# A gated trunk's start, its norm and its banded scores: loads in another order, sums on another engine, rows of 128

## The chip, the cores and the metric

The kernel runs on one core of a Trainium2 chip. The metric is the device time of one execution in microseconds. Engines are named as in the profile: PE is TensorE, DVE VectorE, ACT ScalarE, POOL GpSimd and SP the engine that issues nearly all DMAs. PEld is TensorE's loading of weights, which overlaps its products.

## The reference

Two layers over 512 positions of 1024 features. Each normalises x, modulates it, projects it, runs three causal token mixers side by side, gates and merges them:

```
mod = silu(c) @ w_ada + b_ada;  shift, scale, gate = split(mod, 3)
u = rms_norm(x, norm_g) * (1 + scale) + shift
z = u @ w_in                                 # all mixers' q, k, v and gates
ya = top-k sparse attention (8 heads, rotary, indexer of 4 heads, top 128)
yb = sliding window of 128, 8 q heads on 2 kv heads, sinks in the softmax, rotary
yc = stick-breaking attention (8 heads)
merged = sum_b sigmoid(m_b) * ((y_b * silu(gate_b)) @ w_br_b)
x = x + gate * (merged @ w_out)
```

and a last rms_norm follows. In the banded mixer (b) a block of 128 queries sees its own and the previous block of keys.

## The kernel before

**Tiling.** Features lie on the 128 partitions, positions along the row, so x is eight chunks of 128 x 512 in two tiles, `vc` (chunks 0 to 3) and `va` (4 to 7). Each product of full precision is three of fp32r: a value is split in a high and a low part (u into `uh` and `ul`, weights into `whi` and `wlo`), and hi·hi, hi·lo and lo·hi are summed in PSUM. The first block of a layer (`first_phase`) takes the eight chunks one after another and fills seven banks: 7 x 3 products a chunk. In layer 0, chunks 0 and 1 are worked in halves of 256 positions, 7 x 3 x 2 x 2 = 84 short products, and chunks 2 to 7 whole, 126 products of 512 columns.

**The start** (`start`, with `norm`, `ada_load`, `ada_first`). Before that block, x must be loaded, squared, summed over features (`nones` is a matrix of -1 that sums over partitions), and turned into 1/rms by Ln and Exp on ScalarE; silu(c) is spread into `csr`; and for each chunk j two dot products of 1024 elements (shift and scale: `Y` tiles of w_ada against `csr`, on VectorE) give `mods` and `amul`. `times_rstd` scales x in place and `make_u` makes uh, a copy e and ul. `norm` is called for positions 0 to 255 and again for 256 to 511. Loads go through four `wstage` tiles for weights and five `Y` tiles.

**Who orders the work.** Instructions are recorded by `Recorder.add`, which finds dependencies from the bytes that a view spans (`View.region`: from the lowest to the highest byte), and placed by `Recorder.forward`, a list scheduler: it walks forward in time with a price for each operation, picks an engine where several are allowed (`rec.add` with a dict), and takes the instruction with the earliest start, then the earliest due time of the round before. The best of five rounds is emitted. So every engine's order, SP's queue of loads too, follows from recorded dependencies and prices. All instructions are recorded on one line (549; 547 for products on 64 rows).

**Banded scores** (`softmax_qk`, b = "b"). For a pair of heads the queries lie in `Q`, high part on 64 partitions and low part on the other 64; `kb` is a pair of KH tiles, high and low keys, each with the same 64 rows on both halves. Four blocks of queries by two heads give eight products on 128 rows (high keys against high and low queries) and then, in one run (`low_parts` with `LOW_BAND`), eight on 64 rows (low keys against high queries), two of them side by side on the array. There are four pairs in each of two layers: eight groups.

Of the kernel before, what the change touches and what calls it, by code (L numbers as in the profile page):

```python
# [25 lines left out]
F32 = mybir.dt.float32  # L26
F32R = mybir.dt.float32r
BF16 = mybir.dt.bfloat16
AF = mybir.ActivationFunctionType
OP = mybir.AluOpType  # L30

D = 1024
S = 512
P = 128
# [119 lines left out]
class View:  # L154
# [30 lines left out]
    def real(self):  # L185
# [2 lines left out]
            ap = ap.rearrange(arg, a=more[0]) if more else getattr(ap, name)(arg)  # L188
        return ap

    def region(self):

        whole = self.tile.at
        p0, f0 = divmod(self.at.__array_interface__["data"][0] - whole.__array_interface__["data"][0], whole.shape[1])
        free = list(zip(self.at.strides[1:], self.at.shape[1:]))
        lo = f0 + sum(min(0, s * (n - 1)) for s, n in free)
        hi = f0 + sum(max(0, s * (n - 1)) for s, n in free) + 1
        return p0, p0 + self.at.shape[0], lo, hi
# [45 lines left out]
class Recorder:  # L244
# [29 lines left out]
    def add(self, ways):  # L274
        x = Instr()
        x.i = len(self.list)
        op, args, kw = next(iter(ways.values()))
        if op == "pairs":
            named = [(("out", "in", "in")[n], v) for q in args for n, v in enumerate(q)]
        else:  # L280
            named = [("out" if "out" not in kw and n == 0 else n, v) for n, v in enumerate(args)] + list(kw.items())
        x.writes = [v for n, v in named if isinstance(v, View) and n in ("out", "accum_out")]
        x.reads = [v for n, v in named if isinstance(v, View) and n not in ("out", "accum_out")]
        x.preds, x.succs = {}, []
        for views, w in ((x.reads, False), (x.writes, True)):
            for v in views:
                t, r = v.tile, v.region()
                if op == "matmul" and w and kw["start"]:
                    r = (r[0], r[1], 0, S)
                keep = []  # L290
                for (j, r2, w2) in t.seen:
                    over = r[0] < r2[1] and r2[0] < r[1] and r[2] < r2[3] and r2[2] < r[3]
                    if over and j is not x and (w or w2):
                        x.preds[j.i] = j
                    if not (w and over and r[0] <= r2[0] and r2[1] <= r[1] and r[2] <= r2[2] and r2[3] <= r[3] and j is not x):
                        keep.append((j, r2, w2))
                t.seen = keep + [(x, r, w)]
        x.tiles = list({id(v.tile): v.tile for v in x.reads + x.writes if not v.tile.pool.fixed}.values())
        for j in x.preds.values():
            j.succs.append(x)  # L300
        x.alts = {}
        for e, (op, args, kw) in ways.items():
            x.alts[e] = self.price(x, e, op, args, kw)
        x.prio = x.i
        self.list.append(x)
# [266 lines left out]
def trunk(ctx, tc, xT, vecs, w_ss, w_gt, w_first, w_t, w_v, w_br, w_o, rope, consts, out):  # L572
# [24 lines left out]
    def mm(o, lhsT, rhs, start, stop=True):  # L597
        PE.matmul(o, lhsT, rhs, start=start, stop=stop, skip_group_check=True)
# [5 lines left out]
    f = lambda ap: ap.bitcast(F32)  # L604
# [14 lines left out]
    def both(out, a, b, op_):  # L619
        how = ("tensor_tensor", (), dict(out=out, in0=a, in1=b, op=op_))  # L620
        rec.add({"DVE": how} if in_psum(a, b) else {"POOL": how, "DVE": how})
# [12 lines left out]
    csb, o = small[:, 0:8], 8  # L634
    g_sb = [small[:, o + 8 * l:o + 8 * l + 8] for l in range(L)]
    fg_sb, o = small[:, o + 8 * L:o + 8 * L + 8], o + 8 * L + 8
    b_ada, o = [small[:, o + 24 * l:o + 24 * l + 24] for l in range(L)], o + 24 * L
    sink, o = small[:, o:o + 8 * L], o + 8 * L
    ident = small[:, o:o + P]
    nones = fixed("nones", [P, P], F32R)  # L640
# [56 lines left out]
    st = {}  # L697


    mods = [fixed(f"mods{l}", [P, 24], F32) for l in range(L)]  # L700
    amul = [fixed(f"amul{l}", [P, 8], F32) for l in range(L)]
# [21 lines left out]
    def ada_first(j):  # L723
        o = rec.tile("dot", [P, 4], F32)
        for i in range(2):
            w, m = st["wada", j][i], 8 * i + j
            DVE.scalar_tensor_tensor(w, w, 1.0, csr, op0=OP.mult, op1=OP.mult, accum_out=o[:, i:i + 1])
            DVE.tensor_tensor(out=mods[0][:, m:m + 1], in0=o[:, i:i + 1], in1=b_ada[0][:, m:m + 1], op=OP.add)
        DVE.scalar_tensor_tensor(amul[0][:, j:j + 1], mods[0][:, 8 + j:9 + j], 1.0, g_sb[0][:, j:j + 1], op0=OP.add, op1=OP.mult)

    def ada_g(l, j, q):
        def fn(w):
# [35 lines left out]
    def make_u(l, k, xk, cs_=FULL):  # L768
        t = t512("e", 2)[:, cs_]
        sc, sh = amul[l][:, k:k + 1], mods[l][:, k:k + 1]  # L770
        if cs_.start == 0:
            st["uh"][k] = t512(f"uh{k}", 1, F32R)
            st["ul"][k] = t512(f"ul{k}", 1, F32R)
        for o in (st["uh"][k][:, cs_], t):
            rec.add({"ACT": ("activation", (o, xk[:, cs_], AF.Identity), dict(scale=sc, bias=sh)),
                     "DVE": ("tensor_scalar", (o, xk[:, cs_], sc, sh), dict(op0=OP.mult, op1=OP.add))})
        both(st["ul"][k][:, cs_], t, f(st["uh"][k][:, cs_]), OP.subtract)
# [278 lines left out]
    def low_parts(q, kl, pos, banks, b, order):  # L1056

        quads = []
        for e, i in order:
            k0, W = keys(b, i)  # L1060
            bk, c0 = pos(e, i)
            hp = (H0, H1)[e]
            quads.append((banks[bk][:, c0:c0 + W], q[hp, e, 128 * i:128 * i + 128], kl[hp, k0:k0 + W]))
        pairs(quads)

    LOW_ALL = ((0, 3), (1, 3), (0, 2), (1, 2), (0, 1), (1, 0), (0, 0))
    LOW_BAND = ((0, 2), (1, 2), (0, 3), (1, 3), (0, 1), (1, 1), (0, 0), (1, 0))

    def c_qk(p):
        def fn():  # L1070
# [62 lines left out]
    def softmax_qk(b, p):  # L1133
        def fn():
            q = st[f"{b}q{p}"]
# [8 lines left out]
            for i in (3, 2, 0, 1) if b == "a" else (2, 3, 1, 0):  # L1144
                ts = slice(128 * i, 128 * i + 128)
                k0, W = keys(b, i)
                o, first = [None] * 2, [False] * 2
                for e in es:
                    bk, c0 = pos(e, i)
                    if banks[bk] is None:  # L1150
                        banks[bk], pt[bk], first[e] = sbank(), t512("t", 10), True
                    o[e] = banks[bk][:, c0:c0 + W]
                if b == "a":
                    kh, kl = st[f"ak{p}"]
                else:
                    kh, kl = st["kb"]
                    kv = p // 2
                for e in es:
                    mm(o[e], q[:, e, ts], kh[:, e if b == "a" else kv][:, k0:k0 + W], first[e])
                if b == "a" and i == 1:  # L1160
                    mm(o[1], q[:, 1, ts], kl[:, S:], False)
            if b == "a":
                low_parts(q, kl, pos, banks, b, LOW_ALL)
            else:
                low_parts(q, kl[:, kv], pos, banks, b, LOW_BAND)
            for i in (3, 2, 0, 1) if b == "a" else (2, 3, 1, 0):
                k0, W = keys(b, i)
                if b == "a":
# [250 lines left out]
    def start():  # L1419
# [9 lines left out]
        for h in range(2):  # L1429
# [3 lines left out]
            mm(p, f(nones), d, True)  # L1433
            ACT.activation(csr[:, S * h:S * h + S], p, AF.Copy, scale=-1.0)
        POOL.tensor_scalar(sk8, sink, 8.0, None, op0=OP.mult)
        xx = [rec.tile(t, [P, 4, S], F32) for t in ("vc", "va")]
        x = st["x"] = [xx[k // 4][:, k % 4] for k in range(KT)]
        nb = st["nbank"] = st["rstd"] = sbank()

        def norm(cs_):  # L1440
            for k in range(0, KT, 2):
                SP.dma_start(xx[k // 4][:, k % 4:k % 4 + 2, cs_], xT[:, k:k + 2, cs_])
            prev = None
            for k in range(0, KT, 2):
                t = t512("t", 10)
                a, b = t[:, :S // 2], t[:, S // 2:]
                ACT.activation(t.rearrange("p (a b) -> p a b", a=2), xx[k // 4][:, k % 4:k % 4 + 2, cs_], AF.Square)
                if cs_.start == 0:
                    if k:
                        DVE.tensor_tensor(out=t, in0=t, in1=prev, op=OP.add)  # L1450
                    if k == 6:
                        DVE.tensor_tensor(out=a, in0=a, in1=b, op=OP.add)
                        mm(nb[:, cs_], f(nones), a, True)
                else:
                    both(a, a, b, OP.add)
                    mm(nb[:, cs_], f(nones), a, False, k == 6)
                prev = t
            rstd_of(nb[:, cs_])

        def busy(n, v):  # L1460
# [64 lines left out]
    pos = 0  # L1525
# [71 lines left out]
```

## Time and profile before

| | |
|---|---|
| median of 3 runs | 1230.9 us (1229.34 to 1233.75) |
| profiled execution | 1230.21 us |
| its span | 1228.4 us |
| mean granted TensorE clock | 0.992 |
| TensorE busy | 1197.8 us |
| VectorE busy | 978.2 us |
| ScalarE busy | 553.4 us |
| DMA | 139.40 MB, mean 113 GB/s |

The profiled execution's own time is the span and the little around it. A busy TensorE is one that has a product under way; its products overlap, so a row's duration is longer than the step from one start to the next, and the steps are what adds up.

### The profile page before, as it was taken

To read this page: it belongs to the slowest core of one execution; us is meant where nothing else is said; L and a number is where in the kernel's file an instruction comes from. 1 tells how busy PE (TensorE), PEld (TensorE's weight loads), DVE (VectorE), ACT (ScalarE), POOL (GpSimd) and SP (SyncE) were. 2 spreads that over 40 slices of the span, in tenths; PEclk is the share of its full clock that TensorE was granted. 3 is DMA by queue.
4 is the path that set the end of the run, shared out by engine and by line. 5 is a ranking of instruction groups with operands and counts; after the bars stand their busy time and mean duration, and the time that the engine had idled before them with its cause. 6 is when DMAs were issued, how large, how long until landed. Compare 5 with 4: busy or idle time off the path is not lost.

```text
span 1228.4 us, 17793 instructions
## 1 busy us (share of the span) xinstructions
PE 1197.8 (98%) x5984; PEld 971.8 (79%) x5984; DVE 978.2 (80%) x2142; ACT 553.4 (45%) x1152; POOL 254.3 (21%) x283
## 2 busy tenths in 40 slices
PE   5999999999999999999999999999999999999997
PEld 4889877777877887778898987777777778877886
DVE  7976999999888977777475689989997888667654
ACT  4442767555355532542143157665434554234222
POOL 0110344522111111001200015553220110100120
PEclk7999999999999999999999999999999999999999
DMA  9544222233333555343534432224342224322343
GB/s 341 172 120 136 78 78 86 86 113 113 112 102 96 143 150 144 95 120 123 183 117 104 120 106 77 79 77 114 101 129 78 85 87 113 98 66 78 94 122 102
DMA packets 81915, 139.40 MB, mean 113 GB/s; under 512 B 10016, under 2 KB 22560, under 8 KB 81824
## 3 DMA queue, kind: packets, MB, share of 16 engines
q1 hardware_dynamic: 80672, 136.17, 37.7%
q10 hardware_dynamic: 1152, 2.10, 0.5%
q8 instruction: 47, 0.77, 0.3%
q14 instruction: 44, 0.36, 0.1%
HBM read 125.39 MB, written 4.19 MB: 105 GB/s over the span
## 4 chain that ended last, share of the span: by engine, by line
PE 90%; DVE 4%; DMA 2%; ACT 2%; SPq 1%; issue 0%; DVEq 0%
PE ps_z L549 67%; PE ps_s L549 22%; DVE t L549 2%; ACT t L549 1%; PE ps_s L547 1%; DMA vc<-in_xT 1%; SPq L549 1%; DMA m<-zs 1%; DMA Y<-in_w_ss 1%; DVE Q L549 0%; DVE m L549 0%; DVE wlo L549 0%; DVE e L549 0%; DVE zc L549 0%; DVE score L549 0%
## 5 line engine op out<-in xcount | busy, mean ns | idle before, releaser
L549 PE MATMUL ps_z<-uh,whi 128*128 128x512 f32 (+1 forms) x908 | 360.5, 398 | 8.6 <-ACT uh L549 7.6
L549 PE MATMUL ps_z<-uh,wlo 128*128 128x512 f32 (+1 forms) x908 | 356.1, 393 | 0.0
L549 PE MATMUL ps_z<-ul,whi 128*128 128x512 f32 (+1 forms) x908 | 355.8, 392 | 0.0
L549 POOL TENSOR_TENSOR wlo<-wstage,whi 128x512 fp32r<-128x512 f32 (+2 forms) x134 | 176.8, 1320 | 691.0 <-DVE whi L549 333.7
L549 PEld LDWEIGHTS ps_z<-uh,whi 128*128 128x128 f32 x908 | 170.5, 188 | 48.9 <-ACT uh L549 8.1
L549 PEld LDWEIGHTS ps_z<-uh,wlo 128*128 128x128 f32 x908 | 170.8, 188 | 39.1 <-issue 1.0
L549 PEld LDWEIGHTS ps_z<-ul,whi 128*128 128x128 f32 x908 | 170.9, 188 | 36.0 <-issue 1.1
L549 DVE TENSOR_TENSOR wlo<-wstage,whi 128x512 fp32r<-128x512 f32 (+2 forms) x238 | 156.8, 662 | 11.8 <-ACT whi L549 2.6
L549 ACT CAST whi<-wstage 128x512 fp32r<-128x512 f32 (+2 forms) x145 | 86.0, 596 | 171.6 <-PE ps_z L549 113.1
L549 DVE CAST whi<-wstage 128x512 fp32r<-128x512 f32 (+2 forms) x181 | 74.3, 411 | 111.2 <-PE ps_z L549 93.9
L549 PE MATMUL ps_z<-Y,whi 128*128 128x512 f32 x384 | 121.7, 396 | 0.0
L549 ACT ACTIVATE e<-ps_z 128x512 f32<-128x512 f32 x68 | 40.3, 594 | 129.2 <-PE ps_z L549 128.8
L549 PEld LDWEIGHTS ps_z<-Y,whi 128*128 128x128 f32 x384 | 71.7, 188 | 17.0
L549 ACT ACTIVATE e<-e 128x512 f32<-128x512 f32 x96 | 60.5, 632 | 49.4 <-DVE e L549 48.3
L549 PE MATMUL ps_z<-Y,wlo 128*128 128x512 f32 x192 | 75.8, 395 | 0.0
L549 ACT ACTIVATE t<-t 128x512 f32<-128x512 f32 x120 | 71.1, 628 | 8.2 <-POOL t L549 3.1
L549 ACT ACTIVATE t<-t,nm 128x256 f32<-128x256 f32 (+3 forms) x128 | 65.1, 510 | 17.5 <-DVE nm L549 17.2
L549 PE MATMUL ps_s<-small,t 128*128 128x128 f32 x432 | 59.0, 274 | 6.4 <-DVE t L549 3.9
L549 PEld LDWEIGHTS ps_s<-small,t 128*128 128x128 f32 x432 | 50.0, 141 | 17.9 <-DVE t L549 6.0
L549 POOL CAST whi<-wstage 128x512 fp32r<-128x512 f32 (+1 forms) x46 | 28.9, 629 | 161.6 <-PE ps_z L549 83.5
L549 DVE SCALAR_TENSOR_TENSOR wstage<-wstage,csr 128x512 f32<-128x512 f32 x64 | 50.5, 790 | 6.0 <-DMA wstage<-in_w_ss 4.0
L549 DVE MAX8 m<-score 128x8 f32<-128x256 f32 (+2 forms) x96 | 53.4, 556 | 1.6
(212 smaller groups left out, 2058.0 us busy)
## 6 DMA issues: line engine op xcount, KB each, us to landing
wstage<-in_w_t SPq DMA_DIRECT2D x212, 256.0 KB, 2.7
wstage<-in_w_v SPq DMA_DIRECT2D x48, 182.0 KB, 2.4
Y<-in_w_ss SPq DMA_DIRECT2D x16, 512.0 KB, 7.5
m<-zs SPq DMA_DIRECT2D x128, 64.0 KB, 2.0
wstage<-in_w_gt SPq DMA_DIRECT2D x32, 256.0 KB, 2.6
wstage<-in_w_ss SPq DMA_DIRECT2D x32, 256.0 KB, 2.7
wstage<-in_w_o SPq DMA_DIRECT2D x32, 256.0 KB, 2.7
wstage<-in_w_first SPq DMA_DIRECT2D x16, 256.0 KB, 3.2
```

The source lines that it names most:

```text
L547: self.real[engine].matmul(*[real(a) for a in q], start=False, stop=True, skip_group_check=True)
L549: getattr(self.real[engine], y.op)(*[real(a) for a in y.args], **{k: real(v) for k, v in y.kw.items()})
```

## The change

Four edits.

1. A view of several runs with gaps between them (`x[:, 0:2, 0:256]`) now reports each run as a region of its own, so the two halves of positions of a chunk pair no longer count as overlapping.
2. The squares' sums over chunks are no longer made by VectorE ahead of the product with `nones`; each chunk's square is multiplied by itself and PSUM adds up: eight products a half.
3. `mods` and `amul` of layer 0 are one linear step each, on ScalarE or VectorE as the scheduler finds, with b_ada and the gain folded into `gb` once; uh and e of layer 0 are made by ScalarE only.
4. In the banded mixer the low keys' products use both halves of rows (high and low queries) and stand directly behind the high keys' products of the same block. The full mixers keep their runs on 64 rows.

```diff
+    def regions(self):
+
+        if len(self.at.shape) == 3 and 1 < self.at.shape[1] <= 8 and self.at.strides[1] > self.at.shape[2] * self.at.strides[2] > 0:
+            return [self[:, n].region() for n in range(self.at.shape[1])]
+        return [self.region()]
...
         for views, w in ((x.reads, False), (x.writes, True)):
-            for v in views:
-                t, r = v.tile, v.region()
+            for v, r in [(v, r) for v in views for r in v.regions()]:
+                t = v.tile
...
     def ada_first(j):
         o = rec.tile("dot", [P, 4], F32)
         for i in range(2):
-            w, m = st["wada", j][i], 8 * i + j
+            w = st["wada", j][i]
             DVE.scalar_tensor_tensor(w, w, 1.0, csr, op0=OP.mult, op1=OP.mult, accum_out=o[:, i:i + 1])
-            DVE.tensor_tensor(out=mods[0][:, m:m + 1], in0=o[:, i:i + 1], in1=b_ada[0][:, m:m + 1], op=OP.add)
-        DVE.scalar_tensor_tensor(amul[0][:, j:j + 1], mods[0][:, 8 + j:9 + j], 1.0, g_sb[0][:, j:j + 1], op0=OP.add, op1=OP.mult)
+        g = g_sb[0][:, j:j + 1]
+        linear(mods[0][:, j:j + 1], o[:, 0:1], None, b_ada[0][:, j:j + 1])
+        linear(amul[0][:, j:j + 1], o[:, 1:2], g, st["gb"][:, j:j + 1])
...
         for o in (st["uh"][k][:, cs_], t):
+            if l == 0:
+                ACT.activation(o, xk[:, cs_], AF.Identity, scale=sc, bias=sh)
+                continue
...
                 for e in es:
                     mm(o[e], q[:, e, ts], kh[:, e if b == "a" else kv][:, k0:k0 + W], first[e])
-                if b == "a" and i == 1:
+                if b == "b":
+                    for e in es:
+                        mm(o[e], q[:, e, ts], kl[:, kv, k0:k0 + W], False)
+                elif i == 1:
                     mm(o[1], q[:, 1, ts], kl[:, S:], False)
             if b == "a":
                 low_parts(q, kl, pos, banks, b, LOW_ALL)
-            else:
-                low_parts(q, kl[:, kv], pos, banks, b, LOW_BAND)
...
             for k in range(0, KT, 2):
                 t = t512("t", 10)
-                a, b = t[:, :S // 2], t[:, S // 2:]
                 ACT.activation(t.rearrange("p (a b) -> p a b", a=2), xx[k // 4][:, k % 4:k % 4 + 2, cs_], AF.Square)
-                if cs_.start == 0:
-                    if k:
-                        DVE.tensor_tensor(out=t, in0=t, in1=prev, op=OP.add)
...
-                    mm(nb[:, cs_], f(nones), a, False, k == 6)
-                prev = t
+                for i in range(2):
+                    mm(nb[:, cs_], f(nones), t[:, 256 * i:256 * i + 256], cs_.start == 0 and k + i == 0, k + i == 7)
             rstd_of(nb[:, cs_])
```

On SP, behind the first ada pair (`Y_113`, `Y_116`), the queue of before reads as follows; `vc` and `va` from `in_xT` are the second half of x, `Y` from `in_w_ss` the ada data, `wstage` the weights.

```order
L549 DMA wstage_120<-in_w_first 128x512
L549 DMA wstage_123<-in_w_first 128x384
L549 DMA Y_129<-in_w_ss 128x2x512
L549 DMA Y_134<-in_w_ss 128x2x512
L549 DMA wstage_138<-in_w_first 128x512
L549 DMA wstage_144<-in_w_first 128x384
L549 DMA vc_100<-in_xT 128x2x256
L549 DMA Y_150<-in_w_ss 128x2x512
L549 DMA va_107<-in_xT 128x2x256 x2
L549 DMA Y_170<-in_w_ss 128x2x512
```

And at the same place now:

```order
L555 DMA wstage_122<-in_w_first 128x512
L555 DMA wstage_125<-in_w_first 128x384
L555 DMA vc_101<-in_xT 128x2x256 x2
L555 DMA va_108<-in_xT 128x2x256 x2
L555 DMA Y_147<-in_w_ss 128x2x512
L555 DMA Y_151<-in_w_ss 128x2x512
L555 DMA wstage_155<-in_w_first 128x512
L555 DMA wstage_159<-in_w_first 128x384
```

All four loads of the second half have moved ahead of the second ada pair and the second pair of weights; before, one stood behind both, two more behind a further `Y`, and the last behind the end of this piece.

On ScalarE, from the first half's uh to the second half's Exp (the second `ps_s<-ps_s` row); before:

```order
L549 ACTIVATE uh_195<-vc,mods_72,amul_74 128x256
L549 ACTIVATE e<-vc,mods_72,amul_74 128x256
L549 CAST whi<-wstage 128x512
L549 CAST whi<-wstage 128x384
L549 ACTIVATE t<-vc 128x512
L549 ACTIVATE t<-va 128x512 x2
L549 ACTIVATE t<-vc 128x512
L549 ACTIVATE e<-vc,mods_72,amul_74 128x256
L549 ACTIVATE uh_284<-vc,mods_72,amul_74 128x256
L549 ACTIVATE ps_s<-ps_s,epst 128x256
L549 ACTIVATE ps_s<-ps_s 128x256
```

And now:

```order
L555 ACTIVATE uh_203<-vc,mods_72,amul_74 128x256
L555 ACTIVATE e<-vc,mods_72,amul_74 128x256
L555 ACTIVATE t<-vc 128x512
L555 ACTIVATE t<-va 128x512 x2
L555 CAST whi<-wstage 128x512
L555 ACTIVATE ps_s<-ps_s,epst 128x256
L555 CAST whi<-wstage 128x384
L555 ACTIVATE ps_s<-ps_s 128x256
L555 ACTIVATE uh_278<-vc,mods_72,amul_74 128x256
L555 ACTIVATE e<-vc,mods_72,amul_74 128x256
```

The squares (`t`) now stand ahead of the casts of the second pair of weights, and Ln and Exp stand between and behind these casts, ahead of chunk 1's uh.

On TensorE, the first group of banded scores, before (two heads, so two banks, per block of queries):

```order
L549 MATMUL ps_s_2528<-KH_2310,Q_2479 128x256
L549 MATMUL ps_s_2531<-KH_2310,Q_2479 128x256
...
L549 MATMUL ps_s_2537<-KH_2310,Q_2479 128x256
L549 MATMUL ps_s_2539<-KH_2310,Q_2479 128x256
...
L547 MATMUL ps_s_2528<-KH_2336,Q_2479 128x256
L547 MATMUL ps_s_2531<-KH_2336,Q_2479 128x256
```

And now (`KH_2307` high keys, `KH_2338` low keys):

```order
L555 MATMUL ps_s_2528<-KH_2307,Q_2471 128x256
L555 MATMUL ps_s_2530<-KH_2307,Q_2471 128x256
L555 MATMUL ps_s_2528<-KH_2338,Q_2471 128x256
L555 MATMUL ps_s_2530<-KH_2338,Q_2471 128x256
...
L555 MATMUL ps_s_2547<-KH_2307,Q_2471 128x256
L555 MATMUL ps_s_2549<-KH_2307,Q_2471 128x256
```

A block's low products no longer wait for the high products of all blocks; all sixteen are of one form.

## Rows read from the trace of the kernel before

**Rows 1.** Page, busy time, share of the span and instructions of each engine

```profile
PE 1197.8 (98%) x5984; PEld 971.8 (79%) x5984; DVE 978.2 (80%) x2142; ACT 553.4 (45%) x1152; POOL 254.3 (21%) x283
```

**Rows 2.** Stretches: length, busy PE, PEld, DVE, ACT, POOL; clock, DMA share, GB/s

```profile
0.00:10.00 10.00, 5.55 (x21) 4.26 (x22) 4.78 (x12) 4.98 (x8) 1.30 (x8) 1.00 0.79 258
10.00:18.00 8.00, 7.07 (x45) 6.64 (x45) 7.55 (x20) 4.64 (x9) 0.00 (x0) 0.79 1.07 379
18.00:26.00 8.00, 0.39 (x4) 0.19 (x2) 6.54 (x16) 2.87 (x5) 0.00 (x0) 0.71 1.06 382
26.00:34.00 8.00, 7.93 (x36) 7.01 (x37) 5.05 (x15) 1.91 (x4) 0.00 (x0) 0.65 0.93 338
```

**Rows 3.** Chain that ended last, first 70 us: start, length, what

```profile
9.42 7.23 DMA vc<-in_xT
...
16.66 7.50 DMA vc<-in_xT
...
31.16 0.46 ACT ps_s L549
...
31.64 0.38 ACT ps_s L549
...
32.50 0.61 ACT uh L549
...
33.15 0.51 PE ps_z L549 x2
...
35.70 0.95 PE ps_z L549 x8
```

**Rows 4.** Timeline of PE, end of the first block: start, length, instruction

```profile
67.04 0.39 PE L549 MATMUL ps_z<-uh,wlo 128*128 128x512 f32 x1
67.31 0.66 PE L549 MATMUL ps_s<-small,zs 128*128 128x128 f32 x4
```

**Rows 5.** DMA issues of the first 70 us: KB each, median us to landing

```profile
Y<-in_w_ss SPq DMA_DIRECT2D x16, 512.0 KB, 7.5
wstage<-in_w_first SPq DMA_DIRECT2D x8, 256.0 KB, 5.8
wstage<-in_w_first SPq DMA_DIRECT2D x8, 192.0 KB, 6.4
vc<-in_xT SPq DMA_DIRECT2D x4, 256.0 KB, 5.2
```

**Rows 6.** One stretch of a microsecond

```profile
5.00:6.00 1.00, 1.00 (x4) 0.38 (x2) 0.48 (x2) 0.51 (x1) 0.00 (x0) 1.00 0.95 288
```

**Rows 7.** Timeline of ACT, two casts

```profile
15.38 1.06 ACT L549 CAST whi<-wstage 128x512 fp32r<-128x512 f32 x2 [0.72 <-DMA wstage<-in_w_first]
```

**Rows 8.** Timeline: a dot and a wlo on DVE, four products with nones

```profile
9.64 1.22 DVE L549 SCALAR_TENSOR_TENSOR Y<-Y,csr 128x1024 f32<-128x1024 f32 x1
...
12.51 0.69 DVE L549 TENSOR_TENSOR wlo<-wstage,whi 128x512 fp32r<-128x512 f32 x1
...
27.51 3.62 PE L549 MATMUL ps_s<-t,nones 128*128 128x256 f32 x8
```

**Rows 9.** Timeline of PE, a banded group (L547: 64 rows)

```profile
236.29 1.04 PE L549 MATMUL ps_s<-KH,Q 128*128 128x256 f32 x8
...
236.41 0.52 PE L549 MATMUL ps_s<-KH,Q 128*128 128x256 f32 x3
...
237.06 0.27 PE L549 MATMUL ps_s<-KH,Q 128*128 128x128 f32 x1
237.26 0.68 PE L547 MATMUL ps_s<-KH,Q 64*128 64x256 f32 x8
237.87 0.51 PE L549 MATMUL ps_z<-uh,whi 128*128 128x512 f32 x1
238.21 0.40 PE L549 MATMUL ps_z<-ul,whi 128*128 128x512 f32 x1
```

**Rows 10.** What PE waited for, 800 to 900 us: total, times, longest

```profile
PE ps_s L549 <- DVE t L549: 2.0, 1, 2.0
```

More of the change, by code (lines that the diff above doesn't have):

```diff
@@ L725, in ada_first, with linear @@
         for i in range(2):
-            w, m = st["wada", j][i], 8 * i + j
+            w = st["wada", j][i]
             DVE.scalar_tensor_tensor(w, w, 1.0, csr, op0=OP.mult, op1=OP.mult, accum_out=o[:, i:i + 1])
-            DVE.tensor_tensor(out=mods[0][:, m:m + 1], in0=o[:, i:i + 1], in1=b_ada[0][:, m:m + 1], op=OP.add)
-        DVE.scalar_tensor_tensor(amul[0][:, j:j + 1], mods[0][:, 8 + j:9 + j], 1.0, g_sb[0][:, j:j + 1], op0=OP.add, op1=OP.mult)
+        g = g_sb[0][:, j:j + 1]
+        linear(mods[0][:, j:j + 1], o[:, 0:1], None, b_ada[0][:, j:j + 1])
+        linear(amul[0][:, j:j + 1], o[:, 1:2], g, st["gb"][:, j:j + 1])
+    def linear(o, x, scale, bias):
+        if scale is None:
+            rec.add({"ACT": ("activation", (o, x, AF.Identity), dict(bias=bias)), "DVE": ("tensor_tensor", (), dict(out=o, in0=x, in1=bias, op=OP.add))})
+        else:
+            rec.add({"ACT": ("activation", (o, x, AF.Identity), dict(bias=bias, scale=scale)), "DVE": ("tensor_scalar", (o, x, scale, bias), dict(op0=OP.mult, op1=OP.add))})
     def ada_g(l, j, q):
@@ L1066, in trunk @@
     LOW_ALL = ((0, 3), (1, 3), (0, 2), (1, 2), (0, 1), (1, 0), (0, 0))
-    LOW_BAND = ((0, 2), (1, 2), (0, 3), (1, 3), (0, 1), (1, 1), (0, 0), (1, 0))
     def c_qk(p):
@@ L1435, in start @@
         POOL.tensor_scalar(sk8, sink, 8.0, None, op0=OP.mult)
+        gb = st["gb"] = fixed("gb", [P, 8], F32)
+        DVE.scalar_tensor_tensor(gb, b_ada[0][:, 8:16], 1.0, g_sb[0], op0=OP.add, op1=OP.mult)
         xx = [rec.tile(t, [P, 4, S], F32) for t in ("vc", "va")]
@@ L1442, in norm @@
                 SP.dma_start(xx[k // 4][:, k % 4:k % 4 + 2, cs_], xT[:, k:k + 2, cs_])
-            prev = None
             for k in range(0, KT, 2):
                 t = t512("t", 10)
-                a, b = t[:, :S // 2], t[:, S // 2:]
                 ACT.activation(t.rearrange("p (a b) -> p a b", a=2), xx[k // 4][:, k % 4:k % 4 + 2, cs_], AF.Square)
-                if cs_.start == 0:
-                    if k:
-                        DVE.tensor_tensor(out=t, in0=t, in1=prev, op=OP.add)
[L1451 to L1455, printed above, removed]
-                    mm(nb[:, cs_], f(nones), a, False, k == 6)
-                prev = t
+                for i in range(2):
+                    mm(nb[:, cs_], f(nones), t[:, 256 * i:256 * i + 256], cs_.start == 0 and k + i == 0, k + i == 7)
             rstd_of(nb[:, cs_])
```

## The prediction

> **What bounds the kernel now.** The page's busy line comes first: TensorE is busy 98% of the span [rows 1], so time can come only out of its few gaps or its own work. The table of stretches shows the largest gap: from 18 to 26 us TensorE is busy 0.39 of 8 us, and from 26 to 34 us it works at a mean granted clock of 0.65, mostly the lower level, 1.2 GHz [rows 2]. The chain of waits, read next, tells what that gap waits for: 7.23 and then 7.50 us of DMA, both loads of the second half of x, the last landing at 24.16. Behind it come the second half's norm (Ln, Exp), its uh and, at 33.15, the second half's first products [rows 3]. From there TensorE runs without a gap; the block's last product starts at 67.04 and the next stage's first at 67.31 [rows 4]; with a step of 0.23 the block ends at 67.27. So the first block is bound by the order of its loads until 33.15 and by TensorE afterwards.
>
> **The input, moved forward.** I count bytes in SP's order, 0.262 MB for 256 KB [rows 5]. Before, up to the last load of x stand 1.049 (x) + 1.049 (Y) + 0.459 (two weight loads) + 1.049 (Y) + 0.459 + 0.262 (x) + 0.524 (Y) + 0.524 (x) + 1.049 (Y) + 0.459 + 0.262 (x) = 7.14 MB. The queues moved 2.58 MB in the first 10 us, 3.03 in the next 8, and 0.382 a us after 18 us [rows 2]: 7.96 MB by 24.16. A load thus lands when 0.82 MB more than its own place has moved. Afterwards the last x load stands at 1.049 + 1.049 + 0.459 + 1.049 = 3.61 MB, so it lands at 4.43 MB moved, 14.9 us, 9.3 us earlier. Behind it, and later than before by the 1.05 MB let past, stand the second ada pair (4.66 MB) and the second pair of weight loads (4.92 and 5.11), which land at about 17.6, 18.3 and 18.8 us. Pieces of x are short; in the one microsecond where mostly they moved, the rate was 288 instead of 382 [rows 6], so 1.05 MB costs up to 0.85 us more. I add 0.65 and keep 0 and 0.85 as ends. Weights at 19.0 and 19.5.
>
> ScalarE's new order sets the restart: cast of the first weight load, Ln, cast of the second, Exp, uh of chunk 1. A cast takes about 0.53 (two in 1.06, [rows 7]), Ln 0.46, Exp 0.38, uh 0.61 [rows 3]. From 19.0: cast 19.5, Ln 20.0, cast 20.5 (its load is there at 19.5), Exp 20.9, uh 21.5. VectorE's two dots of the second ada pair (1.22 each [rows 8]) end at about 19.6, so they are no later. Restart at 21.5 instead of 33.15. The moved loads pass the second ada pair and weights in SP's queue; they wait for the landing of loads eight places ahead and for nothing else, so they hold nobody.
>
> **What TensorE has left then.** A 256-wide product costs 0.119 (eight in 0.95 [rows 3]). Before, 33.15 to 67.27 is 34.1 us: 42 such, 5.0, and 126 of 512 columns, 29.1, or 0.231 each. Afterwards only one of the four half tiles is done by 21.5, so 63 short products remain, 7.5 us, and the same 29.1. I add 0.3 where the second half's uh comes 0.3 us behind, and 0.4 where chunk 2's ul stands on VectorE behind four dots in a row. End 21.5 + 7.5 + 29.1 + 0.7 = 58.8 instead of 67.27: **8.5 us gained**. The feeding holds, barely: per further chunk VectorE has two dots, two wlo (up to 0.69) and one ul of about the same, 4.5 us [rows 8], against 21 products at 0.231, 4.85.
>
> **Work that moves.** Squares are now summed by TensorE: 16 products in place of 5. Four of them took 3.62 us at the lower clock [rows 8], so about 0.45 each at the higher: 11 more are 5.0 us. I cost them at nothing, because until 21.5 TensorE waits for loads (the gap of 18 to 26 was empty); without that cover they cost 5.0 at the higher clock and twice that at the lower. VectorE loses the adds of the squares, and most of its small mods and amul steps go to ScalarE, as do all uh and e of the layer. VectorE's saving is hidden, since it waits for the same loads; ScalarE is busy under 5 of 8 us in these stretches [rows 2] and takes it in its gaps. Bounds for these together: minus 1 to plus 2 us.
>
> **The banded mixer.** Eight groups (four pairs, two layers). In one, eight products on 128 rows start at 236.29 and 236.41, so 0.117 for 256 columns; the last starts at 237.06, which after six such leaves 0.07 for one of 128; the first 64-row one at 237.26, the next projection at 237.87, and only the one after, at 238.21, follows in its usual step of 0.23 [rows 9]. So the group costs 238.21 - 0.23 - 236.29 = 1.69 us, of which the changes of form take about 0.13 ahead of the 64-row ones and 0.11 behind them. Sixteen on 128 rows are 12 x 0.117 + 4 x 0.07 = 1.68. I take zero. Ends: the eight 64-row ones at their bare 0.61 against 0.84, plus 0.23 a group, 1.8 us; below, their 0.85 with the changes of form against 0.84, and scores ready about half a microsecond sooner, which VectorE may use in some groups, minus 1.5.
>
> On this the Trainium skill, TensorEngine Tiling (Array Packing), Theoretical Speedup, says that contractions of 64 or fewer rows run up to twice as fast when the array is split; by it alone each group would lose half of 0.84 us, 3.4 in all, and the time would be that of the third rival below. The same page, Key Properties, says that changing the tiling mode drains the engine; the trace agrees [rows 9], with the 0.13 and 0.11 us above, and decides.
>
> On the landing of loads the Trainium skill, DMA: Bandwidth & Descriptors, Queues, rings and completion order, says that each DMA engine takes descriptors in ring order. By strict order without the 0.82 MB every load would land 2.1 us sooner and the gain be 10.6; the trace, with its last x load at 24.16 [rows 3], speaks for the later one.
>
> **The sum.** The profiled execution took 1230.2 (span 1228.4 and 1.8 around it): 1230.2 - 8.5 + 0 = 1221.7. The median shown is 0.7 above that execution, so 1222.4, and I take 1223, since a feed with 0.3 us to spare a chunk loses a little rather than gains. Own range 1219.5 to 1226.5.
>
> **Rivals.** *Late feed.* The second weights land 3 us later than I place them, or VectorE's dots need them in another order. TensorE then stands idle some 4 us from 20 us on; before, the empty stretch from 18 us was followed by a mean clock of 0.65 over 8 us [rows 2], 5.6 of them at half. 3 us late and 2.8 lost at the lower clock leave 2.7 of the gain: 1228. For it: VectorE is 6.5 to 7.5 of 8 us busy there; against it: the bytes, counted above. *No effect.* The loads are asked for early, yet land as late as the ada data that bounds the block anyway: 1230.5. Against it: in before ada data never held VectorE long (the four x pieces held ScalarE). *64 rows were worth it.* The low products on 128 rows cost 0.42 a group more: 1226; the measured changes of form speak against it. *Slower.* In the banded stage VectorE is the second bound: TensorE there waited up to 2.0 us at once for a tile of VectorE's [rows 10]. If the new order of scores puts such a wait into every one of the eight groups, 16 us are lost against 8.5 won: 1238. It decides from 12 us, 1.5 a group; only small parts of TensorE's order move there, which speaks against it.
>
> **Chances.** Forecast 0.71, late feed 0.15 (a fifth of it still faster), no effect 0.05, 64 rows 0.03, slower 0.06. What a measurement here can tell from no change is 0.3%, 3.7 us, so faster means below 1227.2. Faster 0.71 + 0.03 + 0.03 = 0.77, same 0.12 + 0.05 = 0.17, slower 0.06. The range goes from the restart without the short-piece cost and the banded gain (1222.4 - 0.65 - 1.5 - 1, about 1219) to the late feed with a little more lost, 1229.
>
> **What would show it.** The first block's last product ends near 58.8; the last square near 15.5; the second half's Exp near 20.9; no stretch between 21 and 60 us with TensorE idle over 1 us, and the granted clock full there; a banded group of sixteen equal products in 1.7 us. It is wrong if TensorE idles after 20 us, if k-chunks take more than 4.9 us each, or if the banded stages gain waits.

## The result and the profile after

The kernel after took 1220.0 us (median of 6 runs, 1219.4 to 1221.0) against 1229.8 us before (6 runs, 1228.4 to 1233.8): ratio 0.9917, 95% interval [0.9903, 0.9932]. Its profiled execution took 1219.6, its span is 1217.8 us, 10.6 below the span before. (One of the five executions of the kernel called "all but band" below ran at a mean granted clock of 0.85 and took 1308.1 us; its row goes by the other four.)

The busy line of its page, which answers to [rows 1]: TensorE works 2.6 us more in a span 10.6 us shorter, so its idle time fell by 13.2 us, from 30.6 to 17.4; VectorE works 16 us less.

```profile
PE 1200.4 (99%) x6006; PEld 976.3 (80%) x6006; DVE 962.1 (79%) x2106; ACT 556.3 (46%) x1166; POOL 264.3 (22%) x290
```

The stretches, columns as in [rows 2]:

```profile
0.00:10.00 10.00, 8.97 (x36) 7.29 (x36) 2.33 (x9) 4.98 (x8) 1.30 (x8) 1.00 0.81 253
10.00:18.00 8.00, 6.34 (x40) 5.49 (x39) 6.13 (x12) 4.99 (x11) 0.51 (x1) 1.00 1.06 377
18.00:26.00 8.00, 7.97 (x64) 7.60 (x63) 7.89 (x16) 5.99 (x13) 2.22 (x3) 1.00 1.04 381
26.00:34.00 8.00, 8.00 (x48) 7.00 (x47) 7.60 (x15) 4.84 (x9) 0.00 (x0) 1.00 0.91 300
```

The empty stretch is gone: from 18 to 26 us TensorE is busy 7.97 of 8 us where it was 0.39, and the granted clock, 0.79, 0.71 and 0.65 in the three stretches from 10 us on, is now 1.00, the level of 2.4 GHz, in all of them.

ScalarE's timeline between the second half's last squares and the uh that restarts TensorE:

```profile
15.38 1.14 ACT L555 ACTIVATE t<-va 128x512 f32<-128x512 f32 x2
18.71 0.62 ACT L555 CAST whi<-wstage 128x512 fp32r<-128x512 f32 x1 [2.19 <-DMA wstage<-in_w_first]
19.24 0.44 ACT L555 ACTIVATE ps_s<-ps_s,epst 128x256 f32<-128x256 f32 x1
19.61 0.50 ACT L555 CAST whi<-wstage 128x384 fp32r<-128x384 f32 x1
20.01 0.37 ACT L555 ACTIVATE ps_s<-ps_s 128x256 f32<-128x256 f32 x1
20.31 0.58 ACT L555 ACTIVATE uh<-vc,mods,amul 128x256 fp32r<-128x256 f32 x1
```

The last squares start at 15.38 without a wait for x; the cast at 18.71 waits 2.19 us for the second pair of weights, and the Exp, at 31.64 in [rows 3], starts at 20.01. TensorE's timeline at its restart and at the block's end, which answers to [rows 4]:

```profile
15.91 2.75 PE L555 MATMUL ps_s<-t,nones 128*128 128x256 f32 x12
...
20.95 0.51 PE L555 MATMUL ps_z<-uh,whi 128*128 128x256 f32 x2
...
57.60 0.39 PE L555 MATMUL ps_z<-uh,wlo 128*128 128x512 f32 x1
57.83 0.60 PE L555 MATMUL ps_s<-small,zs 128*128 128x128 f32 x4
58.93 0.41 PE L555 MATMUL ps_s<-whi,uh 128*128 128x364 f32 x1 [0.50 <-DVE zc L555]
```

The restart is at 20.95 instead of 33.15, the next stage at 57.83 instead of 67.31: 9.5 us of the 10.6. (A product with `nones` leaves two records, so x12 are six products.)

A banded group on TensorE, which answers to [rows 9]:

```profile
227.59 1.98 PE L555 MATMUL ps_s<-KH,Q 128*128 128x256 f32 x16
229.40 0.44 PE L555 MATMUL ps_z<-uh,whi 128*128 128x512 f32 x1
229.68 0.40 PE L555 MATMUL ps_z<-ul,whi 128*128 128x512 f32 x1
```

By the measure used before, 229.68 - 0.23 - 227.59 = 1.86 us: 0.17 longer than the 1.69 of the group with 64-row products. The row merges two forms, twelve products of 256 columns and four of 128. Of the four, the last three stand here by themselves:

```profile
229.06 0.50 PE L555 MATMUL ps_s<-KH,Q 128*128 128x128 f32 x3
```

They take 229.40 - 229.06 = 0.34 us up to the next product's start, 0.11 each.

### The profile page after: what moved, and what is told of

It reads as the page before. It is cut to its first block, busy times and chain, and to the rows that moved or that the text cites. A ratio compares the mean times of both kernels' runs of the same rounds, so it can differ in the third digit from the quotient of the medians.

```text
span 1217.8 us, 17816 instructions
## 1 busy us (share of the span) xinstructions
PE 1200.4 (99%) x6006; PEld 976.3 (80%) x6006; DVE 962.1 (79%) x2106; ACT 556.3 (46%) x1166; POOL 264.3 (22%) x290
## 4 chain that ended last, share of the span: by engine, by line
PE 89%; DVE 4%; SPq 2%; DMA 2%; ACT 1%; issue 1%; POOL 1%; DVEq 0%; ACTq 0%; POOLq 0%
PE ps_z L555 67%; PE ps_s L555 22%; SPq L555 2%; PE ps_s L553 1%; DMA m<-zs 1%; DVE t L555 1%; DVE Q L555 1%; DVE m L555 1%; DMA wstage<-in_w_first 1%; DMA wstage<-in_w_t 0%; ACT t L555 0%; POOL KH L555 0%; DVE score L555 0%; DVE zc L555 0%; DVE den L555 0%
## 5 line engine op out<-in xcount | busy, mean ns | idle before, releaser
L555 POOL TENSOR_TENSOR wlo<-wstage,whi 128x512 fp32r<-128x512 f32 (+1 forms) x131 | 175.1, 1339 | 662.8 <-DVE whi L555 312.0
L555 ACT CAST whi<-wstage 128x512 fp32r<-128x512 f32 (+2 forms) x141 | 83.4, 596 | 169.7 <-PE ps_z L555 125.9
L555 POOL CAST whi<-wstage 128x512 fp32r<-128x512 f32 (+2 forms) x50 | 31.2, 623 | 134.0 <-PE ps_z L555 63.1
L555 DVE SCALAR_TENSOR_TENSOR wstage<-wstage,csr 128x512 f32<-128x512 f32 x64 | 47.3, 740 | 9.4 <-DMA wstage<-in_w_ss 6.7
```

The source lines that it names most:

```text
L555: getattr(self.real[engine], y.op)(*[real(a) for a in y.args], **{k: real(v) for k, v in y.kw.items()})
```

## The experiments

Edits 1 to 4 are numbered as in the change. "Block's end" is the start of the next stage's first product (`small,zs`), 67.31 before and 57.83 after; spans are 1228.4 and 1217.8. The kernels ran beside before in three groups, in which before took 1230.7, 1229.1 and 1230.1 us; the ratios go by these. Span and block's end come from the one profiled execution, whose time can lie a microsecond or two off the median.

| kernel | edits | median us | ratio to before | span | block's end |
|---|---|---|---|---|---|
| regions only | 1 | 1227.9 | 0.9979 [0.9971, 0.9988] | 1224.1 | 61.37 |
| regions and sums | 1, 2 | 1225.1 | 0.9956 [0.9943, 0.9970] | 1223.3 | 61.65 |
| regions and steps | 1, 3 | 1224.1 | 0.9950 [0.9936, 0.9964] | 1223.1 | 61.45 |
| all but band | 1, 2, 3 | 1221.7 | 0.9931 [0.9917, 0.9944] | 1219.3 | 57.48 |
| all but regions | 2, 3, 4 | 1226.0 | 0.9968 [0.9957, 0.9978] | 1224.2 | 66.73 |
| sums on VectorE | 1, 3, 4 | 1223.0 | 0.9943 [0.9930, 0.9956] | 1221.5 | 59.75 |
| steps on VectorE | 1, 2, 4 | 1223.0 | 0.9949 [0.9937, 0.9961] | 1220.3 | 61.34 |
| band only | 4 | 1228.3 | 0.9985 [0.9976, 0.9994] | 1226.2 | 67.14 |

**Edit 1 alone.** The kernel before with the one change to dependencies (and `regions` as in the change):

```diff
-            for v in views:
-                t, r = v.tile, v.region()
+            for v, r in [(v, r) for v in views for r in v.regions()]:
+                t = v.tile
```

> The kernel before with the first edit alone: a view of several runs reports each run by itself. Theory (the order of the loads is the gain): the four second-half loads of x stand directly behind the first weight pair, the last square comes near 15.4 us instead of 24.2, the first block ends at 58 to 61 us instead of 67.3, and the whole is 7 to 9 us under before. Rival one (the sums on TensorE are needed too, since they keep it busy and its clock up while the loads come): TensorE is idle again between 10 and 20 us, the granted clock falls to 1.2 GHz for several us, the block ends at 62 to 64 us and only 3 to 5 us are gained. Rival two (the banded mixer carries part): 2 to 3 us less than the whole change's 9.8, whatever the start does.

Measured: 1227.9 us, and the block ends at 61.37. My theory falls on the total: 2.8 us under before instead of 7 to 9. The second half's Ln and Exp on ScalarE and TensorE's restart:

```profile
18.28 0.45 ACT L555 ACTIVATE ps_s<-ps_s,epst 128x256 f32<-128x256 f32 x1 [3.14 <-PE ps_s L555]
18.76 0.37 ACT L555 ACTIVATE ps_s<-ps_s 128x256 f32<-128x256 f32 x1
...
20.62 0.39 PE L555 MATMUL ps_z<-uh,whi 128*128 128x256 f32 x1 [1.31 <-ACT uh L555]
```

The Exp starts at 18.76 and TensorE restarts at 20.62, both somewhat earlier than in the kernel after; so the order of loads alone brings the restart. But VectorE then delivers the block's inputs too slowly. From 30 to 58 us, first this kernel, then after:

```profile
30.00:58.00 28.00, 25.47 (x107) 19.38 (x106) 27.18 (x56) 9.42 (x16) 6.38 (x6) 1.00 0.67 217
```

```profile
30.00:58.00 28.00, 28.00 (x124) 22.62 (x123) 23.40 (x43) 16.04 (x31) 5.64 (x7) 1.00 0.72 247
```

With edit 1 alone VectorE is busy 27.18 of 28 us and TensorE idle 2.53; in after VectorE is idle 4.60 us and TensorE not at all. VectorE's timeline in the kernel with edit 1 alone, from the dots of one chunk to those of the next and the next:

```profile
33.93 1.22 DVE L555 SCALAR_TENSOR_TENSOR Y<-Y,csr 128x1024 f32<-128x1024 f32 x1
...
36.53 1.12 DVE L555 TENSOR_TENSOR mods<-dot,small 128x1 f32<-128x1 f32 x1
...
38.96 0.54 DVE L555 TENSOR_SCALAR e<-va,amul,mods 128x512 f32<-128x512 f32 x1
...
40.49 1.22 DVE L555 SCALAR_TENSOR_TENSOR Y<-Y,csr 128x1024 f32<-128x1024 f32 x1
...
43.97 1.52 DVE L555 TENSOR_SCALAR e<-va,amul,mods 128x512 f32<-128x512 f32 x1
...
46.48 1.22 DVE L555 SCALAR_TENSOR_TENSOR Y<-Y,csr 128x1024 f32<-128x1024 f32 x1
```

A chunk takes VectorE 6.56 and 5.99 us, while its 21 products take TensorE 4.85. Two steps in these rows are long: the one on `mods` at 36.53, where the like at 35.19 took 0.16 us, and the copy e at 43.97. Both started while GpSimd made a `wlo`:

```profile
36.07 1.56 POOL L555 TENSOR_TENSOR wlo<-wstage,whi 128x512 fp32r<-128x512 f32 x1 [14.93 <-ACT whi L555]
...
43.83 1.37 POOL L555 TENSOR_TENSOR wlo<-wstage,whi 128x512 fp32r<-128x512 f32 x1 [2.08 <-ACT whi L555]
```

The two hold VectorE about 0.96 and 0.98 us longer than their likes. Without that the chunks would take some 5.6 and 5.0 us, an estimate from these rows: still above 4.85, but by less. So the added steps and GpSimd's work at that moment share in the shortage. In after the same stretch of VectorE:

```profile
38.14 1.21 DVE L555 SCALAR_TENSOR_TENSOR Y<-Y,csr 128x1024 f32<-128x1024 f32 x1
...
42.81 1.22 DVE L555 SCALAR_TENSOR_TENSOR Y<-Y,csr 128x1024 f32<-128x1024 f32 x1
```

4.67 us, just below 4.85: most steps on `mods` and `amul` and the copies e went to ScalarE, and no scaling of x falls in this stretch.

**All but edit 1.**

```diff
-            for v, r in [(v, r) for v in views for r in v.regions()]:
-                t = v.tile
+            for v in views:
+                t, r = v.tile, v.region()
```

> The whole change without its first edit: the second-half loads of x stay where they were. Theory: the last x load lands near 24 us again, and with the sums on TensorE the block ends no sooner than before (67 us) or up to 2 us later; total within 2 us of before. Rival one (sums on TensorE): 3 to 5 us under before. Rival two (banded mixer): 2 to 3 us under before, with the block ending as before.

Measured: 1226.0 us, block's end 66.73. The empty stretch is back:

```profile
18.00:26.00 8.00, 1.28 (x3) 1.11 (x4) 5.08 (x11) 2.87 (x5) 0.00 (x0) 0.68 1.06 381
```

So the order of loads is what fills that stretch, and without it edits 2 and 3 bring the block's end forward by only 0.6 us. My expectation of within 2 us of before misses all the same: the total is some 4 us under it, of which the block and the gap behind it give 1.5 (TensorE resumes for good at 67.14 instead of 68.60) and the later stages, edit 4 among them, the rest.

**Edit 4 alone, and all but edit 4.** The first is the kernel before with this change, the second the kernel after without it:

```diff
+                if b == "b":
+                    for e in es:
+                        mm(o[e], q[:, e, ts], kl[:, kv, k0:k0 + W], False)
...
-            else:
-                low_parts(q, kl[:, kv], pos, banks, b, LOW_BAND)
```

> The kernel before with the banded edit alone. Theory (a group costs 1.68 us in place of 1.69): within 1 us of before, and TensorE's idle time in 200 to 400 and 800 to 1000 us stays at 7 us within 1.5. Rival two (scores are ready sooner and VectorE, the second bound there, uses it): 1.5 to 3 us under before, and that idle time falls by as much. Third rival of the prediction (64 rows were worth it): 3 us over before.

> The whole change without the banded edit. Theory: within 1 us of the whole change, 9 to 10.5 us under before. Rival two: 1.5 to 3 us slower than the whole change, 7 to 8 under before. Third rival of the prediction: 3 us faster than the whole change.

Measured: alone 1228.3 us, with a span 2.2 us below that of before; all but it 1221.7, with a span 1.5 us above that of after. Alone it is clear of the spread; beside the other three the two intervals overlap. Two more pairs of kernels in the table differ by edit 4 alone ("regions and steps" and "sums on VectorE", "regions and sums" and "steps on VectorE"). By the ratios the four pairs give 1.8, 1.7, 0.9 and 0.9 us, all one way: the edit is worth 1 to 2 us, nearer to rival two than to the theory, though its group is 0.17 us longer on TensorE.

From 70 us on, where the banded stages lie, TensorE's idle time falls from 16.9 to 13.9 us with edit 4 alone, and from 15.9 to 13.2 beside the other three; its busy time grows by 0.8 and 1.3. (Over the whole span the fall with edit 4 alone is 30.6 to 25.4, but 2.1 us of it lie in the first 34 us, which the edit does not touch.) What TensorE waited for from 800 to 1000 us (total, times, longest), with all edits but this one, then in after:

```profile
PE ps_s L555 <- DVE t L555: 2.1, 4, 1.0
PE ps_s L555 <- ACT t L555: 0.3, 1, 0.3
PE ps_z L555 <- ACT e L555: 0.3, 1, 0.3
```

```profile
PE ps_z L555 <- DVE xm L555: 1.2, 1, 1.2
PE ps_s L555 <- ACT t L555: 0.3, 1, 0.3
PE ps_s L555 <- DVE t L555: 0.3, 1, 0.3
```

The waits for VectorE's tiles of scores (`t`) shrink from 2.1 to 0.3 us; a wait of 1.2 for `xm` comes in their place. From 70 us to the end the same waits for `t` fall from 4.6 to 0.5 us in this pair and from 3.9, the 2.0 of [rows 10] among them, to 0.5 with edit 4 alone, and those for `xm` rise from nothing to 2.2 and 2.7.

**Sums back on VectorE.** After, with the squares added as before:

```diff
...
-                for i in range(2):
-                    mm(nb[:, cs_], f(nones), t[:, 256 * i:256 * i + 256], cs_.start == 0 and k + i == 0, k + i == 7)
+                if cs_.start == 0:
+                    if k:
+                        DVE.tensor_tensor(out=t, in0=t, in1=prev, op=OP.add)
...
+                else:
+                    both(a, a, b, OP.add)
+                    mm(nb[:, cs_], f(nones), a, False, k == 6)
...
```

> The whole change with its second edit undone: VectorE and GpSimd add the squares again, TensorE makes 5 products instead of 16. Theory now (the moved loads unblock the start, then VectorE's feeding of chunks 3 to 5 is the next bound, and it is the third edit that lifts it): block ends between 57 and 59.5 us, total within 1.5 us of the whole change. Rival one (the sums on TensorE carry the gain, by keeping it busy and off VectorE): the block ends at 60 to 62 us with TensorE idle in 34 to 60 us, total 3 us over the whole change.

Measured: 1223.0 us, 3 us over the whole change, and block's end 59.75. Both miss my theory's bounds, by little at the block's end; the total is the first rival's, but not its idle TensorE later on. Two stretches, and TensorE's restart:

```profile
10.00:18.00 8.00, 6.85 (x42) 6.72 (x42) 6.62 (x16) 5.47 (x12) 1.34 (x1) 0.79 1.07 375
18.00:26.00 8.00, 6.14 (x36) 5.69 (x35) 6.87 (x15) 4.97 (x11) 1.82 (x2) 0.79 1.06 388
```

```profile
9.35 0.67 PE L555 MATMUL ps_s<-t,nones 128*128 128x256 f32 x2 [2.62 <-DVE t L555]
...
21.60 0.50 PE L555 MATMUL ps_z<-uh,whi 128*128 128x256 f32 x2 [1.86 <-ACT uh L555]
```

TensorE idles 2.62 us ahead of the first half's sum and 1.86 ahead of the restart, which comes 0.65 us later than in after, and the granted clock is 0.79 from 10 to 26 us. From 30 to 58 us it is never idle. So edit 2 works at the start, not on the feed. From the restart to the block's end pass 38.15 us, 1.3 more than in after (36.88), with TensorE never idle.

**Steps back on VectorE.** After, with the small steps, uh and e of layer 0 as before:

```diff
-            if l == 0:
-                ACT.activation(o, xk[:, cs_], AF.Identity, scale=sc, bias=sh)
-                continue
...
-        linear(mods[0][:, j:j + 1], o[:, 0:1], None, b_ada[0][:, j:j + 1])
-        linear(amul[0][:, j:j + 1], o[:, 1:2], g, st["gb"][:, j:j + 1])
+            DVE.tensor_tensor(out=mods[0][:, m:m + 1], in0=o[:, i:i + 1], in1=b_ada[0][:, m:m + 1], op=OP.add)
+        DVE.scalar_tensor_tensor(amul[0][:, j:j + 1], mods[0][:, 8 + j:9 + j], 1.0, g_sb[0][:, j:j + 1], op0=OP.add, op1=OP.mult)
...
```

> The whole change with its third edit undone: mods and amul are three steps on VectorE again, uh and e of layer 0 go to either engine. Theory: VectorE is starved for time as with the first edit alone, TensorE is idle 2 to 3 us between 34 and 60 us, the block ends at 60 to 61.5 us and the total is 2 to 4 us over the whole change. Rival one: as the whole change, within 1 us.

Measured: 1223.0 us, block's end 61.34, as the theory had it. From 30 to 58 us TensorE is idle again, 1.82 us, with VectorE at 26.89 of 28:

```profile
30.00:58.00 28.00, 26.18 (x110) 19.86 (x109) 26.89 (x58) 9.61 (x16) 4.33 (x6) 1.00 0.69 224
```

The clock is 1.00 from the start. So edit 3 works on the feed, not at the start.

**Edit 1 with edit 2, and edit 1 with edit 3.** To part the two without edit 4: the kernel with edit 1 alone, with the hunk of the squares' sums, or with that of the steps, as in the change.

> Edits 1 and 2 alone on the kernel before: loads early, squares summed by TensorE, small steps and part of uh and e still on VectorE, banded part as before. Theory (the early restart is used only as far as VectorE feeds the block, and each edit that relieves VectorE buys part of it; the sums also keep TensorE at the full clock until 26 us): block's last product near 59.5, between 61.1 of edit 1 alone and 57.3 of edits 1 to 3; granted clock 1.00 from 10 to 26 us; total near 1225.5. Rival (the sums only matter through the clock and edit 3 does all the relief of VectorE): clock 1.00, but TensorE still starved from 34 to 60 us by 2 us or more, block's last product at 61, total near 1228.

> Edits 1 and 3: loads early, small steps and all uh and e of layer 0 on ScalarE, squares' sums on VectorE, banded part as before. Theory (relief of VectorE and the clock each give part): granted clock 0.79 from 10 to 26 us as in the other kernel with VectorE's sums, TensorE without a gap from 34 to 60 us, block's last product near 59.5, total near 1225. Rival (edit 3 alone gives all of it): block's last product at 57.5 to 58, total near 1222.

Measured: 1225.1 and 1224.1 us, the block ending at 61.65 and 61.45. With edits 1 and 2:

```profile
10.00:18.00 8.00, 7.34 (x44) 6.28 (x43) 6.78 (x15) 4.10 (x8) 0.51 (x1) 1.00 1.07 377
...
34.00:42.00 8.00, 6.91 (x31) 5.38 (x30) 7.85 (x16) 2.89 (x5) 3.27 (x4) 1.00 0.91 290
```

and with edits 1 and 3:

```profile
10.00:18.00 8.00, 6.55 (x33) 6.00 (x33) 6.48 (x13) 5.15 (x11) 1.35 (x1) 0.57 1.06 376
...
34.00:42.00 8.00, 8.00 (x36) 6.53 (x36) 7.66 (x14) 4.25 (x8) 2.65 (x5) 1.00 0.92 339
```

With edit 2 alone beside edit 1 the start runs at 1.00 and TensorE starves later, as the first rival had it, and the block ends no sooner (61.65 against 61.37). With edit 3 alone nothing starves, but the clock is 0.57 from 10 to 18 us and the restart comes at 23.28:

```profile
23.28 0.39 PE L555 MATMUL ps_z<-uh,whi 128*128 128x256 f32 x1 [1.86 <-ACT uh L555]
```

How much edit 3 buys by itself depends on the execution. The kernel with the sums on VectorE has the same edits at the start, and in these two profiles every engine and SP's loads go in the same order until 90 us; yet there the first half's sum comes at 9.35 instead of 9.86, the clock is 0.79 instead of 0.57, the restart comes at 21.60 and the block ends at 59.75 instead of 61.45. So by the block's end edit 3 alone buys between nothing and 1.6 us, and edits 2 and 3 together 3.9 (57.48). Each removes one of two limits that stand one behind the other. My theory had each buy part of the block's end, near 59.5; it falls for edit 2, and for edit 3 two executions disagree.

The same shows in the times of single executions of the kernel with edits 1 and 3: 1221.8, 1223.7, 1224.1, 1224.8 and 1226.4 us at mean granted clocks of 0.997, 0.995, 0.994, 0.994 and 0.992. The six of after lie between 0.997 and 0.999 and within 1.6 us of each other. The total moves less evenly than the block's end: both kernels come out nearer to the theory's 1225 than their blocks do, and what makes the later stages a microsecond or two shorter there is not shown.

**Half the second half's sums.** After, with each pair of squares of positions 256 to 511 added on VectorE or GpSimd, four products less on TensorE:

```diff
+                if cs_.start:
+                    both(t[:, :256], t[:, :256], t[:, 256:], OP.add)
+                    mm(nb[:, cs_], f(nones), t[:, :256], False, k == 6)
+                    continue
...
```

> The whole change, but in the second half each pair of squares is added on VectorE or GpSimd first, so TensorE makes 4 products there instead of 8; the first half keeps its 8. If the second half's sums lie on TensorE's path (in the whole change they take 2.6 us between 16 and 18.5 us, right ahead of uh's products): block ends 1 to 2 us sooner, total 1 to 2 us under the whole change. If the loads of the second weight pair (near 18.7 us) set the restart anyway: no difference, within 0.7 us. If VectorE's feed is the bound all along: 1 us slower.

Measured: 1222.3 us, ratio 0.9949 [0.9937, 0.9961]; block's end 58.71, restart at 21.59. It doesn't beat after but is 2 to 4 us slower, by the medians and by the ratios. The six products from 15.91 in after have all started by 18.3, while the weights are still on their way (the cast that waits until 18.71), so taking some away wins nothing. In this kernel that cast waits for its load until 19.26, 0.55 later, and the restart is 0.64 later: the loads set it, as the second case had it, though its 0.7 us for the total doesn't hold. The rest of the loss lies behind the restart, most of it behind the block, and is not traced.

**More work on VectorE.** After, with one more pass over each `Y` tile of chunks 2 to 7, twelve in all:

```diff
             w = st["wada", j][i]
+            if j >= 2:
+                DVE.tensor_scalar(w, w, 1.0, None, op0=OP.mult)
```

> The whole change with work added on VectorE: each of the two ada tiles of chunks 2 to 7 is multiplied by 1 in place ahead of its dot, 12 steps of about 0.6 us, 7 us in all, the result unchanged. If VectorE's feed is the next bound with 0.3 us to spare a chunk: the block ends 4 to 6 us later, with TensorE idle between 34 and 60 us, and most of it stays in the total. If TensorE bounds the block with more slack than that: 0 to 1.5 us.

Measured: 1231.9 us, ratio 1.0025 [1.0015, 1.0036], slower than before; the block ends at 65.69. One such pass on VectorE's timeline, and the stretch from 30 to 58 us:

```profile
35.18 0.69 DVE L555 TENSOR_SCALAR Y<-Y 128x1024 f32<-128x1024 f32 x1
35.90 1.23 DVE L555 SCALAR_TENSOR_TENSOR Y<-Y,csr 128x1024 f32<-128x1024 f32 x1
```

```profile
30.00:58.00 28.00, 23.98 (x101) 18.24 (x100) 27.42 (x43) 13.56 (x26) 4.86 (x6) 1.00 0.68 214
```

A pass holds VectorE 0.72 us, twelve 8.6; the block ends 7.9 us later. Nearly all of the added work comes through: VectorE's idle time in after gives it little cover, and the feed has next to no slack. The total is 12 us up, twice and more what I expected; some 4 us of it lie behind the block, where nothing was added. What makes them I have not traced.

**VectorE's sums with TensorE kept busy.** As with the sums on VectorE, and eight products into a bank that nobody reads:

```diff
                 if cs_.start == 0:
+                    for i in range(2):
+                        mm(st["warm"][:, :S // 2], f(nones), t[:, 256 * i:256 * i + 256], True)
```

> All four edits but the sums, which stay on VectorE; eight extra products of 256 columns on the first half's squares into a bank that nobody reads, so that TensorE has work between 5 and 10 us. If what the sums on TensorE give is the clock (with VectorE's sums 0.79 from 10 to 26 us, with TensorE's 1.00), the clock rises to 1.00 there, the block ends near 58.3 and the time is 1220.5 to 1221. If what they give is VectorE's time, the block still ends at 59.5 to 60 and the time is near 1222.5.

Measured: 1225.2 us, ratio 0.9960 [0.9947, 0.9972]. The clock is 1.00 from 10 to 26 us, as meant, yet the block ends at 63.47:

```profile
10.00:18.00 8.00, 4.33 (x23) 2.65 (x21) 6.55 (x11) 4.91 (x10) 1.27 (x1) 1.00 1.07 377
18.00:26.00 8.00, 5.60 (x40) 5.01 (x40) 7.08 (x13) 5.25 (x12) 1.87 (x2) 1.00 0.76 262
26.00:34.00 8.00, 8.00 (x57) 8.00 (x56) 7.15 (x13) 4.33 (x10) 1.65 (x3) 0.79 0.78 243
```

The list scheduler answered the added products with another order: the first half's uh reaches TensorE at 20.29 instead of 15.23 in the kernel with the sums on VectorE, and the restart is at 24.92. So this run doesn't part the clock from VectorE's time. The two kernels with VectorE's sums do in part: between restart and block's end, with TensorE never idle, each takes 1.3 us more than after (38.15 and 38.17 against 36.88) at granted clocks of 0.79 and 0.87 from 18 to 26 us, where after has 1.00. That much I put down to the clock. How the later restart, 0.65 us in one and 2.3 in the other, divides between the clock and VectorE's adds stays open.

## Why the prediction was right, and where its steps were not

The total came 3.0 us below the forecast and in its own range, and the mechanism is the one forecast: loads in another order, the restart at the weights' landing, a block bound by TensorE from there.

*Loads.* Weights were placed at 19.0 and 19.5; the cast waits until 18.71 and the next one, at 19.61, waits for nothing. Counting bytes in queue order was right to 0.3 us, and the late feed did not come. The price of the short pieces was too high: by bytes alone the first weights were due at 18.3, so the pieces cost at most some 0.4 us and not 0.65. (By the prediction's own rates its upper end is 0.9, not 0.85.)

*Restart.* 20.95 against 21.5; the Exp ends at 20.38 against 20.9. The casts, Ln and Exp overlap at their ends: the start of one to that of the next is 0.53, 0.37, 0.40 and 0.30, 0.64 from the last to the product, while I added up whole durations of 0.38 to 0.61.

*The block.* From restart to end 36.9 us against 37.3: the products left were counted rightly, and 9.5 us were gained against 8.5.

*The norm on TensorE, and the steps on ScalarE.* TensorE's added products were costed at nothing, and so it is: the last of the second half's starts at 18.28, ahead of the weights. What fell is the price of the edits. "VectorE's saving is hidden, since it waits for the same loads" is wrong: putting the steps back costs 3.5 us at the block's end, putting the sums back 1.9. The feed of the whole change held about as counted, 4.67 us a chunk against 4.5, but only because edit 3 had taken the other steps off VectorE: in the kernel with edit 1 alone VectorE also works on `mods`, e and the scaling of x, 6.0 to 6.6 us a chunk with GpSimd's two holds in them, against 4.85. In the kernel before the same VectorE fed the block without a gap because it had worked ahead while TensorE waited until 33.15: nine of the sixteen dots were made by then, four by the restart at 20.62 with edit 1 alone. My 8.5 us, written under the moved input, needs edits 2 and 3; the move by itself ends the block 5.9 us sooner and makes the run 2.8 us shorter (1227.9 against 1230.7). The total was right because the whole change has all three; for edits that I had put at nothing, that was luck.

*The banded mixer.* Forecast zero between minus 1.5 and plus 1.8; measured minus 1 to minus 2. The term was mis-sized in two places. Sixteen products take 1.86 us and not 1.68, because products of 128 columns were put at 0.07 and three of the four take 0.11, and because 0.05 us more pass behind them. That makes eight groups 1.4 us longer, and the run is 1 to 2 us shorter even so: the shorter waits for `t` bring more than the half a microsecond in some groups that I put at the lower end. On TensorE alone the 64-row form is the faster one, by 0.17 us a group; for the run it is not. The rule of the Trainium skill, TensorEngine Tiling (Array Packing), Theoretical Speedup, that contractions of 64 rows or fewer run up to twice as fast when the array is split, would at its full factor make the group without them 0.42 us longer; the rows here show less than half of that.

*The sum.* Of the 10.6 us of span, 9.5 are the block and 0.2 the shorter gap behind it. The last 0.9 lie in the rest: behind the gap the kernel with edits 1 to 3 takes 0.9 us more than before, and after takes 1.8 less than that kernel. What the loss of 0.9 comes from is not shown. So the 3.0 us between forecast and median are 1.0 of the block, 0.2 of the gap, 0.9 of the rest, 0.6 that I had added to 1222.4 for a feed that loses a little, and 0.3 because after's median lies only 0.4 above its profiled execution, where I had put 0.7.

## What to carry to other kernels

When a late load is moved ahead, the time that TensorE waited for it was also another engine's head start: count every instruction which that engine issues per chunk, small steps and copies too, before calling the block bound by TensorE. Limits that stand one behind the other don't show their worth one at a time (one edit worth nothing by itself at the block's end, the other nothing or 1.6 us by the execution, 3.9 us together), so undo each from the whole as well as adding each to the start. Where a scheduler orders the whole program, an edit in one stage moves others by one or two microseconds; effects of that size need the stage's own rows beside the total.

## What the runs showed of the hardware

- In the kernel with edit 1 alone, a step on one column on VectorE took 1.12 us where its like took 0.16, and a copy e 1.52 where another took 0.54; both stand on the feed that ran short, and both started while GpSimd made a `wlo`. In the first 70 us of the thirteen traces of this case twenty steps of VectorE took over 0.3 us longer than the median of their form. All twenty started while GpSimd made a `wlo` or, once, a `whi`, and ended after it, though not every step that started so was held. The 24 steps that make `G` out of a PSUM tile (`ps_z`) during such a `wlo` took 0.67 to 0.69 us, as ever. No experiment moved GpSimd's work away, so this is a coincidence in time, not a tested cause.
- The granted clock of a stretch didn't go with the busy time of the same stretch: in the last experiment 1.00 from 10 to 26 us at 4.33 and 5.60 busy of 8 us, and then 0.79 from 26 to 34 us at 8.00 of 8.
